# Weights one piece later and a reordered block inverse in the RWKV stage of a hybrid diffusion step

## The chip, the cores and the metric

One core of one Trainium2 chip. The metric is the device time of one launch in microseconds: median 2254.62 us of three runs before the change (2253.39 to 2256.46).

## The reference, cut to what matters

One layer over 640 tokens (512 of a sample, 128 of a prompt), model width 2048. A normed and modulated input goes through one large projection `w_in`; an RWKV-7 branch (16 heads of 64 channels, scanned forward and backward) and an RG-LRU branch run beside each other, are projected, gated, summed, projected once more, added to the input and normed.

```python
def rwkv7_scan(r, w, k, v, kk, a, s0, reverse):
    def step(s, inp):
        r_t, w_t, k_t, v_t, kk_t, a_t = inp
        s_kk = jnp.einsum('bhvk,bhk->bhv', s, kk_t)
        s = s * w_t[:, :, None, :] - s_kk[..., None] * (kk_t * a_t)[:, :, None, :] + v_t[..., None] * k_t[:, :, None, :]
        return s, jnp.einsum('bhvk,bhk->bhv', s, r_t)
    ...
    z = xm @ p['w_in']
    r, k, v, g_a, x_b, g_b, m_a, m_b = jnp.split(z, SPLITS, axis=-1)
    ...
    (y_f, bo_f, s_f), (y_bk, bo_bk, s_bk) = dirs_a
    y_rwkv = head_group_norm((y_f + y_bk)...) + (bo_f + bo_bk).reshape(bsz, t, W_A)
    y_a = (y_rwkv.astype(dt) * jax.nn.silu(g_a)) @ p['w_out_a']
    merged = jax.nn.sigmoid(m_a) * y_a + jax.nn.sigmoid(m_b) * y_b
    out = merged @ p['w_out']
```

The kernel computes the scan in chunks of 64 tokens. Within a chunk the steps form a triangular system (I + A), and the kernel inverts that matrix for each of 10 chunks, 2 directions and 2 heads of a channel tile.

## The kernel before

**Stages.** Modulation and norm, the RG-LRU branch (to about 500 us), the RWKV branch (to about 1765 us), the branches' output projections with the merge, and the last projection with the final norm. Products with weights run on TensorE in float32 as three products of two exact parts each.

**Pieces of weights.** The stream of weights is cut into pieces of 128x512 (4 k-tiles of one column tile, 256 KB). SyncE issues the load of a piece into one of 3 raw tiles `wr` (`fetch`, line 297). `split` turns each half of a piece into a high part `wh` (ScalarE, line 309) and a low part `wl` (GpSimd, line 310), with 5 tiles of each. `piece` (line 327) runs 4 k-tiles on TensorE, 6 matmuls of 320 columns each. Before every half-piece it first splits up to 5 half-pieces ahead and then calls `fetch(pos[1] // 2 + src["raw"])`, so that loads stand 3 pieces ahead of the split in the program.

**Ticks.** After each k-tile comes one tick: it counts down the delayed calls (`later(n, fn)`) and lets three queues of generators (front, side, back) run one step each. `yield from idle(n)` waits n ticks. Ticks fix in which order instructions stand on an engine; each engine then runs its own list strictly in that order and waits where it must. All DMAs spoken of here are issued by SyncE (the rows' SPq), so a load stands behind whatever was issued before it in the program.

**The RWKV stage** has 8 channel tiles, numbered 0 to 7. While `rwkv(i, v)` runs for tile i, the products of the next tile's r, k, v, of a gate and of some merge gates go through the pieces: 28 pieces for each of tiles 1 to 6. For one tile, `rwkv` does in this order:

- `first` (line 968): products whose masked result `at` holds A, forward (d = 0) and then backward (d = 1).
- `send` (line 1011): four DMAs write the 32x32 diagonal blocks of A to DRAM; they are read back with one block on each partition, forward into `xn` (line 1079) and backward into `xi` (line 1098). ScalarE turns the forward blocks (line 1102: `xi` from `xn`) and the backward ones (line 1105: `xn` from `xi`).
- The elimination: 30 steps of two VectorE instructions each (lines 1110 and 1112) invert all blocks, while `second` and `turned` go on TensorE between. The tuples `W` and `INV` hold the ticks between these steps. It ends with a memset of the diagonal (line 1118) and a turned copy to `xn` (line 1119).
- Four DMAs (line 1123) send `xi` and `xn`, each for both directions, to DRAM. `QI[1]` ticks later four small loads (line 1131) bring what the first products need, and eight (line 1137) bring the diagonal blocks of the full inverse `qm`. `QI[2]` ticks after that follow the first products of the inverse (line 1146), copied by ScalarE at line 1152, 3 ticks later the second products (line 1160), copied at line 1166, and then the recurrence over chunks.

Behind the elimination the next tile's `normed` starts: it loads two tiles `th` (line 821) and squares `nk` (line 902).

Of the kernel before, what the change touches and what calls it, by code (L numbers as in the profile page):

```python
# [9 lines left out]
F32 = mybir.dt.float32  # L10
# [6 lines left out]
P = 128  # L17
D = 2048
KT = D // P            # 16 k-tiles of the model dimension
WA = 1024  # L20
NT = WA // P           # 8 channel tiles of a branch
TS = 512               # sample tokens
TP = 128               # prompt tokens
T = TS + TP            # 640 tokens: sample first, then prompt
HT = T // 2            # tokens of one PSUM half
CH = 64                # chunk of the RWKV recurrence
NC = T // CH           # 10 chunks: 8 of the sample, 2 of the prompt
LR = 96
EARLY = 2              # column tiles of w_in among the first products
NS = 3 + EARLY         # and with those of the LoRA branches  # L30
SLOT = 658             # columns of a slot: 640 tokens with the borders of their shifts
NM = (5, 3, 3, 3, 3, 3, 4)          # column tiles of the merge gates among the products of a channel tile
CUT = 350              # tokens of the first group of the output projection
# buffers: parts of weights, the same and raw weights of the last phase, ada_w, gate's weights, slots of the LRU phase
WB, EW, ER, ADAB, GS, LS = 5, 5, 6, 10, 2, 14
# The order in which TensorE takes the work that others wait for, in pieces of the products between its steps.
# start: steps behind each group of ada_w; loads of ada_w before the first weights; place of the derived parameters
LQ = ((), (0, 2, 3, 5, 7), (4, 6, 8), (1, 3, 4, 6, 8), (1, 3, 4, 6, 8), (1, 3, 4, 6, 8), (1, 4, 4, 6, 8), (1, 3, 4, 6, 8))
LF, DN = 2, 0
# LRU phase: LoRA, convolution, gates, recurrence, gate's third of the modulation  # L40
# [3 lines left out]
# RWKV phase: keys' side; chunk products, inverses, recurrence; group norm  # L44
QB, NQ, HP, BC, BG = 21, 7, (4, 3, 3), 5, 2
W = (2, 2, 2, 2, 2, 2, 2, 2, 2, 1, 3, 2)
INV = (0, 1, 1, 1, 1, 1, 1, 1, 2, 2, 2, 2, 2, 2, 2, 2)
QI = (1, 5, 7, 3, 1)
# [4 lines left out]
# output projections  # L53
# [5 lines left out]
# per-channel parameters of the two branches, in the order in which they are packed  # L59
# [3 lines left out]
# columns of the constants  # L63
# [3 lines left out]
HB = CH // 2           # blocks that VectorE inverts  # L67
NB = 4 * NC            # of them in a direction of a channel tile
# [15 lines left out]
def _lay_out(inp):  # L84
    """The inputs as the kernel reads them: transposed, tiled and packed, no arithmetic."""
# [14 lines left out]
    # the column tiles of the first products, in pieces of 2 k-tiles, k-tiles outermost, two to a transfer  # L100
# [5 lines left out]
    # shift and scale: tile of columns, third, group of 4 k-tiles, partition, k-tile, column  # L106
    w = f["ada_w"][0][:, :2 * D].reshape(4, 4, P, 2, KT, P)
    a["ada_w"] = w.transpose(4, 3, 0, 2, 1, 5).reshape(KT, 2, 4, P, 4 * P)
    # gate: half of k, tile of columns, column, k
# [25 lines left out]
def step_kernel(ctx: ExitStack, tc: tile.TileContext, xt, w_in, w_a, w_b, w_o, ws, lw2, ada_w, ada_g, ada_b, cond, condr, gains,  # L135
# [17 lines left out]
    # ---------------------------------------------------------------- constants and parameters  # L153
# [3 lines left out]
    blk = keep.tile([P, P], F32R, name="blk")        # ones between the channels of a head  # L157
# [4 lines left out]
    mod = keep.tile([P, 3, KT, 2], F32, name="mod")      # shift, 1 + scale (times the norm's gain), gate  # L162
# [13 lines left out]
    def derive(pool):  # L176
        V.tensor_scalar(dv[:, 0:3], pt[:, 0:3], -1.0, 1.0, ALU.mult, ALU.add)          # 1 - mu
        V.tensor_scalar(dv[:, 3:6], pt[:, 0:3], 0.25, None, ALU.mult)                  # mu / 4
        V.tensor_scalar(dv[:, 6:9], pt[:, 0:3], 0.5, None, ALU.mult)                   # mu / 2
        kb = PAR.index("dw0")  # L180
        V.tensor_scalar(dv[:, 9:17], pt[:, kb:kb + 8], 0.5, None, ALU.mult)            # halved biases of the sigmoids
        V.tensor_scalar(dv[:, 17], pt[:, PAR.index("k_a")], 0.5, None, ALU.mult)
        V.tensor_scalar(dv[:, 18], pt[:, PAR.index("k_k")], -1.0, None, ALU.mult)
        # 4 softplus(-lambda), softplus(-l) = max(-l, 0) + 2 atanh(e / (2 + e)), e = exp(-|l|)
# [18 lines left out]
    # ---------------------------------------------------------------- side work, between the pieces of the products  # L203
# [43 lines left out]
    # ---------------------------------------------------------------- the stream of weights  # L247
    # Each piece: 4 k-tiles of one column tile, split exactly into two parts of 12 significant bits.
# [41 lines left out]
    src = {"pool": wpool, "raw": 3, "parts": WB}  # L290
# [9 lines left out]
    def split(j):  # L300
        """Parts up to half-piece j."""
        while pos[1] < min(j, 2 * len(stream)):
            k, q = divmod(pos[1], 2)
            r = raws[k][:, 2 * P * q:2 * P * (q + 1)]
            if q:
                raws.pop(k)
            h = src["pool"].tile([P, 2 * P], F32R, tag="wh", name="wh", bufs=src["parts"])
            lo = src["pool"].tile([P, 2 * P], F32R, tag="wl", name="wl", bufs=src["parts"])
            S.activation(h, r, AF.Copy)  # L309
            lows[pos[1] % len(lows)].tensor_tensor(lo, r, h.bitcast(F32), ALU.subtract)  # L310
            parts[pos[1]] = (h, lo)
            pos[1] += 1

    def piece(j, xs, hs, k0, nk, ticks=True, qs=range(4)):
        """p[m, tokens a to b] += (4 k-tiles of the weights)^T @ x, both in two parts, for (p, a, b) of hs."""
        for q in qs:
            if q % 2 == 0:
                split(2 * j + q // 2 + src["parts"])
                fetch(pos[1] // 2 + src["raw"])
# [25 lines left out]
    def newton(x, y, t):  # L345
        """x^-1/2 from x > 0 and the table's value y for it: one step, to y."""
# [8 lines left out]
    # ---------------------------------------------------------------- modulation and the normed input  # L355
# [9 lines left out]
    def ada_load(pool, bufs, t):  # L365
        """Group t of 4 k-tiles of 2 column tiles of ada_w, by pair of column tiles, third and k."""
# [17 lines left out]
    def ada_turn(third, n, ms, psa):  # L384
        """To 2 channel tiles of mod, the four groups of columns summed, with the bias."""
# [6 lines left out]
    with tc.tile_pool(name="start", bufs=1) as st, tc.tile_pool(name="ps", bufs=2, space=PSUM) as sp:  # L392
# [40 lines left out]
        # the first column tiles: two are summed in PSUM, the others in sums  # L433
# [7 lines left out]
        def modulated(n):  # L441
            """The normed and modulated input of 2 channel tiles."""
# [14 lines left out]
        def first(n, c):  # L457
            """Column tile c's products with 2 channel tiles."""
# [62 lines left out]
    # ---------------------------------------------------------------- LoRA branches and the RG-LRU branch  # L521
# [5 lines left out]
    with tc.tile_pool(name="lru", bufs=1) as lp:  # L527
# [19 lines left out]
        def parted(src, name, low, bufs=1):  # L547
            """Two parts of 12 significant bits."""
# [5 lines left out]
        def small(p, w, x):  # L554
            """p = w^T @ x, both in two parts."""
# [43 lines left out]
        def lru(i, xb, sg):  # L599
# [32 lines left out]
            for d in range(2):  # L632
                # log a = -4 sp (1 + th);  1 - a^2 = tanh(-log a) (1 + a^2)
# [38 lines left out]
        def gates():  # L672
            """The gate's third of the modulation: columns on partitions, sums over k along them."""
# [35 lines left out]
        for i in range(NT):  # L709
            side.append(lora(i))  # L710
            xb = slot("xb")
            # sample: 2 zeros, 512, 1 zero; prompt: 2 zeros, 128, 1 zero
# [16 lines left out]
            V.scalar_tensor_tensor(halves(sg), halves(sg), 1.0, ps[:, :, :HT], ALU.add, ALU.mult)   # 2 silu(g_b)  # L729
# [9 lines left out]
    # ---------------------------------------------------------------- the RWKV branch  # L739
# [3 lines left out]
    with tc.tile_pool(name="rwkv", bufs=1) as rp:  # L743
# [3 lines left out]
        def mixed(q, i):  # L747
            """The projection of r, k or v, mixed with its shift."""
# [47 lines left out]
        # (I + A)^-1, transposed, of each chunk: its blocks of 32 from VectorE, the rest from TensorE  # L796
# [4 lines left out]
        NV = 64 + NB       # partitions that hold blocks, backward from 64  # L801
# [620 lines left out]
```

## Time and profile before

| | |
|---|---|
| median of 3 runs | 2254.62 us (2253.39 to 2256.46) |
| span of the profiled execution | 2255.7 us, 1.1 us above the median and within the range of the runs |
| busy: TensorE / VectorE / ScalarE / GpSimd | 94% / 60% / 43% / 39% |
| DMA | 38.9% of 16 engines' time on SyncE's queue |
| chain that ended last | TensorE 67%, VectorE 20%, DMA 4% |

The profile lists busy time, waits ("idle before, and who ended it") and the instructions in order of time. Where an engine's row has [6.05 <-DMA xi<-scr], the engine stood idle for 6.05 us until that DMA landed. A row merges neighbours of one kind: x4 behind it is their number, and its duration runs from the first to the last.

### The profile page before, as it was taken

What the parts mean: (1) busy time and instruction counts of PE and PEld (TensorE: products, weight loads), DVE (VectorE), ACT (ScalarE), POOL (GpSimd) and SP (SyncE); (2) the same over time, 40 slices, a digit from 0 to 9 for tenths busy, and PEclk for the clock granted to TensorE, in tenths of its full rate; (3) what the DMA queues carried; (4) which work ended last, traced back from release to release, by engine and by line L of the source; (5) the groups of instructions that cost most, each with busy time, mean ns of one, the idle gap of its engine ahead of it and who ended that gap; (6) DMA issues with size and microseconds to landing.
All of it is one profiled execution on the core that took longest, in us unless ns stands there. A gap on an engine that the chain in (4) does not pass through costs nothing.

```text
span 2255.7 us, 47335 instructions
## 1 busy us (share of the span) xinstructions
PE 2115.5 (94%) x18236; PEld 1971.3 (87%) x18236; DVE 1346.7 (60%) x2536; ACT 980.9 (43%) x2264; POOL 890.8 (39%) x1164
## 2 busy tenths in 40 slices
PE   4999898999999899898998998989999999999997
PEld 2788898998888889798898897888988899999997
DVE  5557898968856667656756676567362422223364
ACT  4336566653434443433443434334433422234554
POOL 1245555664323333333333433333323444443343
PEclk8999899999999999999999999999999999999999
DMA  8955555432322322322222223222232533345574
GB/s 334 349 175 166 177 174 173 155 101 85 96 82 72 87 70 72 99 78 78 78 83 86 68 76 97 71 74 92 85 90 68 196 122 122 122 143 159 153 237 151
DMA packets 198609, 281.63 MB, mean 125 GB/s; under 512 B 68816, under 2 KB 90512, under 8 KB 197616
## 3 DMA queue, kind: packets, MB, share of 16 engines
q1 hardware_dynamic: 197936, 277.38, 38.9%
q8 instruction: 144, 2.36, 0.4%
q0 software_dynamic: 448, 1.23, 0.2%
q14 instruction: 81, 0.66, 0.1%
HBM read 237.70 MB, written 39.85 MB: 123 GB/s over the span
## 4 chain that ended last, share of the span: by engine, by line
PE 67%; DVE 20%; DMA 4%; issue 2%; ACT 2%; SPq 1%; POOL 0%; DVEq 0%; ACTq 0%; POOLq 0%
PE pj L327 50%; DVE tmp L1110 3%; DVE xi L1112 3%; PE rw L557 2%; PE rw L968 2%; PE rw L473 2%; DVE st L992 2%; DVE xc L611 1%; DMA scr<-xn 1%; PE pj L473 1%; PE rw L1191 1%; PE rw L1179 1%; PE rw L1204 1%; DVE gws L703 1%; PE ada L375 1%
## 5 line engine op out<-in xcount | busy, mean ns | idle before, releaser
L310 POOL TENSOR_TENSOR wl<-wr,wh 128x256 fp32r<-128x256 f32 x922 | 804.5, 880 | 1266.7 <-ACT wh L309 1223.9
L327 PE MATMUL pj<-xh,wh 128*128 128x320 f32 (+2 forms) x2976 | 764.6, 325 | 2.4 <-ACT wh L309 2.4
L327 PE MATMUL pj<-xh,wl 128*128 128x320 f32 (+2 forms) x2976 | 726.2, 312 | 1.9 <-DVE wl L310 1.4
L327 PE MATMUL pj<-xl,wh 128*128 128x320 f32 (+2 forms) x2976 | 726.3, 312 | 0.0
L309 ACT ACTIVATE wh<-wr 128x256 fp32r<-128x256 f32 x1048 | 423.6, 413 | 547.2 <-PE pj L327 421.0
L327 PEld LDWEIGHTS pj<-xh,wh 128*128 128x128 f32 x2976 | 503.3, 190 | 34.3 <-issue 14.2
L327 PEld LDWEIGHTS pj<-xh,wl 128*128 128x128 f32 x2976 | 513.7, 190 | 3.7 <-DVE wl L310 2.1
L327 PEld LDWEIGHTS pj<-xl,wh 128*128 128x128 f32 x2976 | 514.9, 190 | 0.1
L1110 DVE TENSOR_TENSOR tmp<-xn,xi 104x30 f32<-104x30 f32 (+14 forms) x240 | 102.7, 428 | 82.0 <-ACT xn L1105 75.5
L1039 DVE COPY sv<-rw 64x128 f32<-64x128 f32 x80 | 23.6, 294 | 197.2 <-ACT sv L1038 196.1
L310 DVE TENSOR_TENSOR wl<-wr,wh 128x256 fp32r<-128x256 f32 x126 | 58.4, 465 | 125.0 <-ACT wh L309 124.8
L1112 DVE TENSOR_TENSOR xi<-xi,tmp 104x30 f32<-104x30 f32 (+14 forms) x240 | 100.0, 416 | 8.2
L1338 DVE SCALAR_TENSOR_TENSOR thx<-thx,pj 128x640 f32<-128x640 f32 x16 | 13.2, 823 | 95.8 <-PE pj L327 95.8
L992 DVE TENSOR_TENSOR st<-rw,c 64x512 f32<-64x512 f32 (+1 forms) x96 | 57.5, 599 | 12.4 <-PE rw L986 10.2
L327 PE MATMUL pj<-ybh,wl 128*128 128x320 f32 x256 | 58.6, 310 | 0.4 <-POOL wl L310 0.3
L327 PE MATMUL pj<-ybh,wh 128*128 128x320 f32 x256 | 58.5, 310 | 0.0
L327 PE MATMUL pj<-yah,wh 128*128 128x320 f32 x256 | 58.4, 309 | 0.0
L327 PE MATMUL pj<-yah,wl 128*128 128x320 f32 x256 | 58.4, 309 | 0.0
L327 PE MATMUL pj<-yal,wh 128*128 128x320 f32 x256 | 58.3, 309 | 0.0
L327 PE MATMUL pj<-ybl,wh 128*128 128x320 f32 x256 | 58.3, 309 | 0.0
L1146 PE MATMUL rw<-xi,at 32*32 32x32 f32 x640 | 15.0, 231 | 43.4 <-DMA xi<-scr 42.9
L1038 ACT ACTIVATE sv<-rw 64x128 f32<-64x128 f32 x80 | 21.6, 271 | 75.9 <-PE rw L1191 70.2
(766 smaller groups left out, 3168.2 us busy)
## 6 DMA issues: line engine op xcount, KB each, us to landing
wr<-w_in SPq DMA_DIRECT2D x312, 256.0 KB
adaw<-ada_w SPq DMA_DIRECT2D x64, 512.0 KB
wr<-w_o SPq DMA_DIRECT2D x128, 256.0 KB
gws<-ada_g SPq DMA_DIRECT2D x32, 512.0 KB
thl<-th SPq DMA_DIRECT2D x32, 320.0 KB
th<-thl SPq DMA_DIRECT2D x32, 320.0 KB
thm<-g SPq DMA_DIRECT2D x64, 160.0 KB
thx<-thm SPq DMA_DIRECT2D x32, 320.0 KB
```

Source lines behind the costliest of these rows:

```text
L309: S.activation(h, r, AF.Copy)
L310: lows[pos[1] % len(lows)].tensor_tensor(lo, r, h.bitcast(F32), ALU.subtract)
L327: PE.matmul(p[:, :t1 - t0], w, x[:, t0:t1], start=(k == 0 and a == 0), stop=(k == nk - 1 and a == 2))
L375: PE.matmul(pm[32 * q:32 * q + 32, :2 * P].rearrange("p (b c) -> p b c", b=2), sc[:, 4 * g + q], wt[:, :, P * q:P * (q + 1)], start=(g == ...
L473: PE.matmul(p[:, :HT], u[:, w], x[:, t], start=new, stop=end)
L557: PE.matmul(p, a, b, start=(n == 0), stop=(n == 2))
L611: V.scalar_tensor_tensor(xc[:, a:b], xb[:, o + q:o + q + n], pc(f"cw{q}", i), xc[:, a:b], ALU.mult, ALU.add)
L968: PE.matmul(pa[hd(e), x:x + P], z.bk[d][hd(e), n, e], st4s[d][hd(e), n, e].rearrange("p a t -> p (a t)"), start=True, stop=True)
L992: V.tensor_tensor(st4s[d][so, n0:n0 + nn, e], pb[so, :m].rearrange("p (c a t) -> p c a t", a=2, t=CH), mb[so], ALU.mult)
L1039: V.tensor_copy(sv[hd(1), a, 1], src[hd(1), b])
L1110: V.tensor_tensor(t, xn[:NV, j, j + 1:].unsqueeze(2).to_broadcast([NV, m, j]), xi[:NV, j, :j].unsqueeze(1).to_broadcast([NV, m, j]), ALU.mult)
L1112: V.tensor_tensor(xi[:NV, j + 1:, :j], xi[:NV, j + 1:, :j], t, ALU.add)
```

## The change

Four edits in the RWKV stage; the comments fall away too. Loads of weights are called 2 instead of 3 pieces ahead from the start of the RWKV stage to the end of the merge, with the same 3 raw tiles. The forward blocks of A are sent one tick sooner, read back 5 ticks sooner and turned 5 ticks sooner; the backward blocks are sent, read back and turned one tick sooner each, and the elimination starts 2 ticks sooner in the program and gets 2 ticks more. The four sends after it go in another order, and the 12 small loads are called 2 ticks sooner.

```diff
-W = (2, 2, 2, 2, 2, 2, 2, 2, 2, 1, 3, 2)
-INV = (0, 1, 1, 1, 1, 1, 1, 1, 2, 2, 2, 2, 2, 2, 2, 2)
-QI = (1, 5, 7, 3, 1)
+W = (2, 2, 2, 2, 2, 2, 2, 2, 2, 1, 2, 1)
+INV = (0, 1, 1, 1, 1, 1, 1, 2, 2, 2, 2, 2, 2, 2, 2, 3)
+QI = (1, 3, 9, 3, 1)
...
-    src = {"pool": wpool, "raw": 3, "parts": WB}
+    src = {"pool": wpool, "raw": 3, "ahead": 3, "parts": WB}
...
-                fetch(pos[1] // 2 + src["raw"])
+                fetch(pos[1] // 2 + src["ahead"])
...
-            later(2, lambda: send(0))
+            later(1, lambda: send(0))
...
             pb = heads([z.bonus])
+            later(1, lambda: nc.sync.dma_start(xn[0:NB], sa[0][0].rearrange("g n r c -> (g n) r c")))
             yield from idle(W[5])
...
-            later(2, lambda: send(1))
-            later(2, lambda: nc.sync.dma_start(xn[0:NB], sa[0][0].rearrange("g n r c -> (g n) r c")))
+            later(1, lambda: send(1))
+            later(3, lambda: nc.sync.dma_start(xi[64:NV], sa[1][0].rearrange("g n r c -> (g n) r c")))
+            S.activation(xi[0:NB], xn[0:NB].rearrange("p j t -> p t j"), AF.Copy)
...
             yield from idle(W[8])
-            nc.sync.dma_start(xi[64:NV], sa[1][0].rearrange("g n r c -> (g n) r c"))
             next(work)
             yield from idle(W[9])
             next(work)
-            S.activation(xi[0:NB], xn[0:NB].rearrange("p j t -> p t j"), AF.Copy)
             yield from idle(W[10])
-            next(work)
             S.activation(xn[64:NV], xi[64:NV].rearrange("p t j -> p j t"), AF.Copy)
+            next(work)
             yield from idle(W[11])
...
-            for d in range(2):
-                for w, x in ((1, xi), (2, xn)):
-                    nc.sync.dma_start(sa[d][w].rearrange("g n r c -> (g n) r c"), x[64 * d:64 * d + NB])
+            for d, w in ((0, 1), (1, 2), (1, 1), (0, 2)):
+                nc.sync.dma_start(sa[d][w].rearrange("g n r c -> (g n) r c"), (xi, xn)[w - 1][64 * d:64 * d + NB])
...
+        src.update(ahead=2)
         pace[:] = [0.0, 1.0]
         rkv = {}
...
-        src.update(pool=fp, raw=ER, parts=EW)
+        src.update(pool=fp, raw=ER, ahead=ER, parts=EW)
```

Three places in the order of the instructions. The numbers behind names tell the buffers apart; a piece of weights is the same tile `wr_...` on SyncE (its load) and on ScalarE (its split).

SyncE (SP) behind the four sends of tile 1's inverse, before:

```order
L297 DMA wr_8711<-w_in 128x512
L1131 DMA xi_5437<-scr1_0_1_5426 32x10x32 x2
L1131 DMA xi_5437<-scr1_1_2_5430 32x10x32 x2
L1137 DMA qm0_5434<-scr1_0_2_5427 32x10x32 x2
L1137 DMA qm1_5435<-scr1_1_1_5429 32x10x32 x2
L1137 DMA qm0_5434<-scr1_0_2_5427 32x10x32 x2
L1137 DMA qm1_5435<-scr1_1_1_5429 32x10x32 x2
L821 DMA th_8765<-thl2_0_1688 128x640
L821 DMA th_8767<-thl2_2_1690 128x640
L297 DMA wr_8777<-w_in 128x512
```

Ahead of the 12 small loads stands one piece, behind the loads of `th` the next. ScalarE (ACT) at the same place before, from the wait for `nk` to the copies behind the first products:

```order
L902 ACTIVATE q_8771<-nk_8769 128x640
L309 ACTIVATE wh_8773<-wr_8592 128x256
L309 ACTIVATE wh_8791<-wr_8657 128x256
L309 ACTIVATE wh_8807<-wr_8657 128x256
L309 ACTIVATE wh_8825<-wr_8711 128x256
L1152 ACTIVATE xn_5436<-rw_8835 32x320 x2
L1152 ACTIVATE xn_5436<-rw_8836 32x320 x2
```

The piece whose first half ScalarE splits right before line 1152 (wr_8711) is loaded ahead of the 12 small loads. SyncE at the same place now:

```order
L297 DMA wr_8709<-w_in 128x512
L1131 DMA xi_5437<-scr1_0_1_5426 32x10x32 x2
L1131 DMA xi_5437<-scr1_1_2_5430 32x10x32 x2
L1137 DMA qm0_5434<-scr1_0_2_5427 32x10x32 x2
L1137 DMA qm1_5435<-scr1_1_1_5429 32x10x32 x2
L1137 DMA qm0_5434<-scr1_0_2_5427 32x10x32 x2
L1137 DMA qm1_5435<-scr1_1_1_5429 32x10x32 x2
L821 DMA th_8763<-thl2_0_1688 128x640
L821 DMA th_8765<-thl2_2_1690 128x640
L297 DMA wr_8775<-w_in 128x512
```

What stands between the two pieces is unchanged; which pieces they are, ScalarE's rows now tell:

```order
L902 ACTIVATE q_8769<-nk_8767 128x640
L309 ACTIVATE wh_8771<-wr_8655 128x256
L309 ACTIVATE wh_8789<-wr_8709 128x256
L309 ACTIVATE wh_8805<-wr_8709 128x256
L309 ACTIVATE wh_8823<-wr_8775 128x256
L1152 ACTIVATE xn_5436<-rw_8833 32x320 x2
L1152 ACTIVATE xn_5436<-rw_8834 32x320 x2
```

The piece split right before line 1152 is now wr_8775, and its load stands behind the 12 small loads and the two loads of `th`. ScalarE before the elimination of tile 1, before:

```order
L309 ACTIVATE wh_8197<-wr_8010 128x256
L1005 ACTIVATE tok_7889<-rw_8218 128x5x64
L1005 ACTIVATE tok_7889<-rw_8219 128x5x64
L1102 ACTIVATE xi_5437<-xn_5436 40x1024
L309 ACTIVATE wh_8233<-wr_8077 128x256
L1272 ACTIVATE g_8249<-pj_7873 128x320
L309 ACTIVATE wh_8251<-wr_8077 128x256
L1105 ACTIVATE xn_5436<-xi_5437 40x1024
```

The same stretch now (lines 1102 and 1105 have become 1082 and 1104):

```order
L1082 ACTIVATE xi_5437<-xn_5436 40x1024
L1272 ACT_TABLE_LOAD
L1272 ACTIVATE g_8175<-pj_7871 128x320
L309 ACTIVATE wh_8178<-wr_8079 128x256
L309 ACTIVATE wh_8197<-wr_8079 128x256
L1005 ACTIVATE tok_7887<-rw_8217 128x5x64
L1005 ACTIVATE tok_7887<-rw_8218 128x5x64
L309 ACTIVATE wh_8231<-wr_8141 128x256
L1272 ACTIVATE g_8247<-pj_7871 128x320
L1104 ACTIVATE xn_5436<-xi_5437 40x1024
```

The forward turn has moved ahead of a merge gate, two halves of weights and the copies of `tok`, and the backward turn has one instruction of 128x256 less ahead of it.

## Rows read from the trace of the kernel before

**Rows 1.** The page, part 1: the span and TensorE's busy time.
```profile
span 2255.7 us, 47335 instructions
...
PE 2115.5 (94%) x18236; PEld 1971.3 (87%) x18236; DVE 1346.7 (60%) x2536; ACT 980.9 (43%) x2264; POOL 890.8 (39%) x1164
```
**Rows 2.** TensorE's waits: who waited for whom, total us, times, longest us.
```profile
PE rw L1146 <- DMA xi<-scr: 42.9, 16, 6.5
```
**Rows 3.** TensorE's timeline, tile 1 and tile 6: start, duration, instruction, [idle before].
```profile
752.96 0.46 PE L327 MATMUL pj<-xh,wh 128*128 128x320 f32 x2
753.25 0.46 PE L327 MATMUL pj<-xl,wh 128*128 128x320 f32 x2
...
760.04 0.82 PE L1146 MATMUL rw<-xi,at 32*32 32x32 f32 x6 [6.05 <-DMA xi<-scr]
761.21 1.27 PE L1146 MATMUL rw<-xi,at 32*32 32x32 f32 x74 [0.34 <-DMA xi<-scr]
...
762.41 0.90 PE L327 MATMUL pj<-xh,wh 128*128 128x320 f32 x2
...
767.11 0.89 PE L1160 MATMUL rw<-qm,xn 32*32 32x32 f32 x80
...
1522.54 0.89 PE L1160 MATMUL rw<-qm,xn 32*32 32x32 f32 x80
```
**Rows 4.** Busy time and granted clock (PEclk) behind tile 1's first products.
```profile
761.00:767.00 6.00, 5.79 (x92) 5.65 (x92) 0.00 (x0) 2.75 (x6) 3.06 (x4) 0.54 0.55 117
```
**Rows 5.** VectorE's timeline: elimination's start and end, tile 1; its end, tile 6.
```profile
716.47 0.19 DVE L1110 TENSOR_TENSOR tmp<-xn,xi 104x30 f32<-104x30 f32 x1 [9.10 <-ACT xn L1105]
...
752.95 0.09 DVE L1118 MEMSET xi<- 104x32 f32 x1
...
1509.43 0.09 DVE L1118 MEMSET xi<- 104x32 f32 x1
```
**Rows 6.** ScalarE's timeline in tile 1: the turns, the halves, line 1152.
```profile
711.26 2.09 ACT L1102 ACTIVATE xi<-xn 40x1024 f32<-40x1024 f32 x1
...
714.33 2.10 ACT L1105 ACTIVATE xn<-xi 40x1024 f32<-40x1024 f32 x1
...
758.87 1.38 ACT L309 ACTIVATE wh<-wr 128x256 fp32r<-128x256 f32 x4
762.44 1.78 ACT L1152 ACTIVATE xn<-rw 32x320 f32<-32x320 f32 x4 [2.19 <-PE rw L1146]
```
**Rows 7.** SyncE's timeline in tile 1, behind the four sends.
```profile
755.67 0.86 SPq L297 DMA_DIRECT2D wr<-w_in  x1
756.58 3.02 SPq L1131 DMA_DIRECT2D xi<-scr  x4
759.69 4.73 SPq L1137 DMA_DIRECT2D qm<-scr  x8
764.47 0.93 SPq L821 DMA_DIRECT2D th<-thl  x2
765.50 2.19 SPq L297 DMA_DIRECT2D wr<-w_in  x3
```
**Rows 8.** SyncE in tile 6, behind the loads of th: the issue.
```profile
1522.26 1.72 SPq L297 DMA_DIRECT2D wr<-w_in  x3
```
**Rows 9.** ScalarE's halves that waited for a load: tiles 6, 7, end of stage.
```profile
1526.13 0.42 ACT L309 ACTIVATE wh<-wr 128x256 fp32r<-128x256 f32 x1 [0.48 <-DMA wr<-w_in]
...
1677.30 0.42 ACT L309 ACTIVATE wh<-wr 128x256 fp32r<-128x256 f32 x1 [5.62 <-DMA wr<-w_in]
...
1771.70 0.42 ACT L309 ACTIVATE wh<-wr 128x256 fp32r<-128x256 f32 x1 [3.89 <-DMA wr<-w_in]
```
**Rows 10.** SyncE at the end of the stage: the loads behind five loads of yr.
```profile
1765.56 0.85 SPq L297 DMA_DIRECT2D wr<-w_in  x2
```
**Rows 11.** TensorE in tile 0: a wait of the stage, and the second products.
```profile
602.93 0.61 PE L892 MATMUL rw<-qhh,blk 128*128 128x320 f32 x1 [3.04 <-ACT g L1272]
...
619.76 0.89 PE L1160 MATMUL rw<-qm,xn 32*32 32x32 f32 x80
```

More of the change, by code (lines that the diff above doesn't have):

```diff
@@ L1101, in rwkv @@
             next(work)
-            S.activation(xi[0:NB], xn[0:NB].rearrange("p j t -> p t j"), AF.Copy)
             yield from idle(W[10])
+            S.activation(xn[64:NV], xi[64:NV].rearrange("p t j -> p j t"), AF.Copy)
             next(work)
-            S.activation(xn[64:NV], xi[64:NV].rearrange("p t j -> p j t"), AF.Copy)
             yield from idle(W[11])
```

## The prediction, made before the changed kernel ran

> **What bounds the kernel now.** I read the busy shares first: TensorE works 94% of a span of 2255.7 us [rows 1], so time can only go or come where TensorE stands. The list of its waits then names one large wait of the RWKV stage: 42.9 us ahead of the first products of the inverse, for the small loads of line 1131 [rows 2]. In the timeline of tile 1 it is one piece: 6.05 and 0.34 us ahead of line 1146, with the main part of these products at 761.21 and the second products (line 1160) at 767.11 [rows 3]. Tiles 1 to 6 look alike, tiles 0 and 7 are treated apart.
>
> Next I followed that wait back. VectorE ends the elimination at 752.95, and it had stood idle for 9.10 us until the backward turn let it begin at 716.47 [rows 5]. So the elimination starts when ScalarE's line 1105 is done (714.33 + 2.10), and line 1102 (2.09 us at 711.26) stands shortly ahead of that [rows 6]. Behind the elimination SyncE issues, one after another, a piece of weights, 12 small loads, two loads of `th` and the next weights [rows 7]. I count from the end of the elimination before, E = 752.95: small loads from E + 3.6, the load behind `th` at E + 12.6, first products E + 8.3, second products E + 14.2; in tile 6 the second products come at 1522.54 - 1509.43 = 13.1 [rows 3, 5]. As the middle of these six I take E + 13.6.
>
> **The change part by part.**
>
> *Earlier blocks.* Line 1102 leaves the place ahead of the backward turn (2.09 us), and one half of weights goes behind it. On the other side a merge gate and the copies of `tok` still stand ahead of it, so I take 2.2 us for the start of the elimination. The bounds are 0 (its data come no sooner) and 9.10 (all of VectorE's idle time). VectorE has the same 60 steps and the same other work between, so the end moves by as much: E - 2.2.
>
> *Order of the sends.* The third and fourth small load need the backward `xn`, which was sent last and now goes second. The four issues took 3.02 us where eight later ones took 4.73 [rows 7]: 4 x 0.59 = 2.4, so 0 to about 1.2 us can go; I take 0.6. The earlier call of the small loads (`QI[1]`) passes nothing on SyncE in tiles 1 to 6: the same number of weight loads, one, stands between sends and small loads.
>
> By these two parts the first products come at E + 8.3 - 2.8 = E + 5.5. That is 2.8 us of TensorE's wait in each tile, were it all.
>
> *Weights one piece later.* In general I cost this at nothing: there are still 3 raw tiles, a load still waits for the same tile to be free, and the splits run up to five half-pieces ahead. A half-piece is 6 pairs of matmuls at 0.29 us [rows 3], 1.8 us, so five are about 8.8 us of cover. What was queued behind a waiting weight load goes out sooner. What now stands behind other SyncE work is a weight load, and at one place the cover is gone. ScalarE splits a half-piece right ahead of line 1152, the copies that the second products need. Before, that piece was loaded ahead of the 12 small loads (755.67, E + 2.7). Now one piece less has been fetched, and that load is the one behind the small loads and `th` (765.50) [rows 7]. Its issue is E + 12.6 - 2.8 = E + 9.8. In tile 6 the load in this slot was issued at 1522.26 [rows 8] and the half that waited for it began at 1526.13 [rows 9]: 3.9 us. So the piece is there at E + 13.7, the half takes 0.42, line 1152 takes 1.78 [rows 6], and the second products start about 0.1 later, at E + 16.0. Before it was E + 13.6. Each of the six tiles loses 2.4 us, although its first products came 2.8 us sooner: 6 x 2.4 = 14.4 us. Queued behind ScalarE's waiting half are line 1152, the square of the next tile and all later halves; behind TensorE's line 1160 is everything.
>
> The Trainium skill, "DMA: Bandwidth & Descriptors", section "Anatomy of one DMA", fits a transfer as about 2.0 us and its bytes over 436 GB/s, which would be an estimate of 2.6 us for a piece of 256 KB. The row says 3.9 us in this slot, behind two loads of 320 KB, and the measurement decides. By the page the loss would be 1.1 us a tile, 6.6 us in all. The same page's "Rules for kernel authors" say to issue a transfer early and wait for it late, which speaks against this part; how late is too late no page says, and the sum stands without it.
>
> *The clock.* After the idle time of 6 us, TensorE was granted 0.54 of its speed from 761 to 767, the lower of its two levels (1.2 GHz) for most of it [rows 4]. The three k-tiles between first and second products took 767.11 - 762.41 = 4.7 us, against 9 x 0.29 = 2.6 at the upper level (2.4 GHz) [rows 3]: 2.1 us lost, inside the E + 13.6. Now there are two idle times: about 3.6 us (6.39 - 2.8) ahead of the first products, and then, with these done at about E + 6.7 and three k-tiles of 2.6 to 4.7 us, 4.6 to 6.7 us ahead of the second ones. What the clock loses after the first is hidden in the second; after the second nothing hides it. I take 2.1 us again, 6 x 2.1 = 12.6 us, with bounds 0 and 0.46 x 6.0 = 2.8 us a tile.
>
> *Tile 0* has no `th` in between, and loses its wait of 3.04 us at 602.93 in part, as a store comes out sooner; but its second products (619.76) [rows 11] then wait for a load that is also behind the 12 small ones. I take +2 (bounds -3 and +5). *Tile 7*: ScalarE waited 5.62 us for this very load even before [rows 9], when it was issued ahead of the small ones; now it is behind them, while the elimination ends sooner. I take +1 (bounds -1 and +6).
>
> *End of the stage.* Two weight loads at 1765.56 stood behind five loads of `yr` [rows 10], and the split of the first waited until 1771.70 [rows 9]. One piece less is there beforehand, so TensorE runs dry one piece sooner: 12 pairs x 0.29 = 3.5 us. I take +4 with some clock (bounds 0 and +6).
>
> Sum: 14.4 + 12.6 + 2 + 1 + 4 = 34 us on 2255.7. That execution stood 1.1 us above the median of 2254.62, so 2254.6 + 34 = 2288.6, told as 2288 us.
>
> **The rivals.**
>
> 1. *The clock does not fall a second time* (0.22). The shortened first wait may leave it up, or the second end before it falls. For it: the bound of 0. Against: an idle time of 6 us was followed by the low level in rows 4. Time: 2288 - 12.6 = 2275.
>
> 2. *The elimination ends no sooner* (0.09). The backward turn may be held by its data or by the halves ahead. Then the second products come at E + 18.2, 2.2 us later still in six tiles: 2288 + 13 = 2301.
>
> 3. *Gain and loss cancel* (0.06): the load lands in the page's 2.6 us, no second fall of the clock, nothing at the end: 2254.6 + 6.6 - 3 = 2258 and below, about 2255.
>
> 4. *Faster, because the elimination starts much sooner* (0.13). The second products hang on its end: they come as early as before where it ends 2.2 + 2.4 = 4.6 us sooner, and earlier from there. For it: VectorE's 9.10 us of idle time, and a forward turn that now is far ahead, so that only the backward one counts. Against: that one still stands behind a gate and halves of weights that wait for TensorE's own progress, and it moved by one tick only. At 9.10 us the gain is 4.5 us a tile in seven tiles, 31 us, so about 2223; a middle case is 2240.
>
> **How the numbers follow.** The forecast has 0.50, and with rivals 1 and 2 slower has 0.81. A measurement of this kernel tells a change from none at about 0.2%, 4.5 us: same is 2250 to 2259, where rival 3 lies: 0.06. Faster is rival 4: 0.13. The low end takes 6.6 us for the loads, no second clock loss and -3 of tile 0: 2258. The high end takes 2.8 us for the clock (+4), +5, +6 and +6 for the three single places (+10), no gain by the order of the sends (+4): 2306. Outside lie rival 4 and a little of both ends.
>
> **What would show it.** Right: TensorE's wait at line 1146 shrinks to 3 or 4 us a tile; a new wait of 4 to 7 us appears ahead of line 1160; ScalarE's half ahead of the copies of line 1152 is ended by a load of weights; the granted clock is low behind the second products. VectorE's idle time ahead of the elimination is about 7 us instead of 9.10. The last forward pieces of the stage show a longer wait near 1766. Wrong: line 1152 follows the first products at once, as it did, or the elimination starts 5 us or more sooner; then tiles get shorter and the kernel faster.

## The result and the profile after

The changed kernel takes 2295.62 us (median of 4 runs, 2292.84 to 2296.55) against 2255.54 us (2253.39 to 2257.10) for the kernel before: a ratio of 1.017, 95% interval 1.0158 to 1.0183, so about 40 us slower. The forecast was 2288 us, with 2258 to 2306 as its range and slower as the likeliest side. The profiled execution has a span of 2293.5 us, 37.8 more than [rows 1].

TensorE's waits in the changed kernel (who waited for whom, total us, times, longest us), against the one wait of [rows 2]:

```profile
PE rw L1160 <- ACT xn L1152: 38.0, 13, 5.3
PE rw L1146 <- DMA xi<-scr: 25.4, 9, 4.1
...
PE pj L327 <- ACT wh L309: 4.9, 1, 4.9
```

The old wait shrank from 42.9 to 25.4 us, and a new one of 38.0 us stands behind it, ahead of line 1160. In tile 1 TensorE's timeline (start, duration, instruction, [idle before]) shows both, where [rows 3] had one:

```profile
760.27 0.34 PE L1146 MATMUL rw<-xi,at 32*32 32x32 f32 x4 [4.08 <-DMA xi<-scr]
760.77 1.36 PE L1146 MATMUL rw<-xi,at 32*32 32x32 f32 x76 [0.17 <-DMA xi<-scr]
762.06 0.90 PE L327 MATMUL pj<-xh,wh 128*128 128x320 f32 x2
...
765.41 0.46 PE L327 MATMUL pj<-xh,wl 128*128 128x320 f32 x2
770.85 0.29 PE L1160 MATMUL rw<-qm,xn 32*32 32x32 f32 x2 [4.98 <-ACT xn L1152]
771.30 2.17 PE L1160 MATMUL rw<-qm,xn 32*32 32x32 f32 x78 [0.17 <-ACT xn L1152]
```

TensorE runs the three k-tiles between the two products and then stands still for 4.98 us. Behind it line 1160 itself takes 2.17 us where it took 0.89. Who holds it is read from ScalarE's timeline of the same place; [rows 6] has the same instructions before:

```profile
758.32 0.74 ACT L902 ACTIVATE q<-nk 128x640 f32<-128x640 f32 x1 [9.84 <-DVE nk L900]
758.97 0.40 ACT L309 ACTIVATE wh<-wr 128x256 fp32r<-128x256 f32 x1
759.93 0.72 ACT L309 ACTIVATE wh<-wr 128x256 fp32r<-128x256 f32 x2 [0.57 <-DMA wr<-w_in]
769.92 0.42 ACT L309 ACTIVATE wh<-wr 128x256 fp32r<-128x256 f32 x1 [9.27 <-DMA wr<-w_in]
770.36 1.79 ACT L1152 ACTIVATE xn<-rw 32x320 f32<-32x320 f32 x4
```

Before, four halves stood together and line 1152 waited only for TensorE. Now three halves go, and the fourth waits 9.27 us for a load of weights, with line 1152 queued behind it, although its products were done at about 762.1. The load is the first of the three that SyncE issues last here:

```profile
755.76 1.10 SPq L297 DMA_DIRECT2D wr<-w_in  x1
756.91 2.42 SPq L1131 DMA_DIRECT2D xi<-scr  x4
759.42 4.97 SPq L1137 DMA_DIRECT2D qm<-scr  x8
764.43 0.93 SPq L821 DMA_DIRECT2D th<-thl  x2
765.46 1.32 SPq L297 DMA_DIRECT2D wr<-w_in  x3
```

The order on SyncE is that of [rows 7]; what differs is which piece each load of weights brings. The half that waits for the first of these three starts 4.46 us after that load's issue (765.46 to 769.92).

On VectorE the idle time ahead of the elimination is 6.69 us where it was 9.10 [rows 5], and the elimination's end is at 753.02:

```profile
716.26 0.19 DVE L1110 TENSOR_TENSOR tmp<-xn,xi 104x30 f32<-104x30 f32 x1 [6.69 <-ACT xn L1104]
...
753.02 0.09 DVE L1118 MEMSET xi<- 104x32 f32 x1
```

TensorE came to line 1146 at 760.27 - 4.08 = 756.2, so 3.2 us behind that end; before it came at 760.04 - 6.05 = 754.0, 1.0 us behind the end of 752.95. By TensorE's progress the elimination thus ends 2.1 us sooner.

The granted clock stands in the windows (from and to in us, length, busy time of PE, PEld, DVE, ACT, POOL, then PEclk, DMA share, GB/s). In the changed kernel, first between the first and the second products, then behind the second ones:

```profile
762.00:769.00 7.00, 3.87 (x24) 3.54 (x18) 0.00 (x0) 0.00 (x0) 0.00 (x0) 0.85 0.65 169
...
771.70:778.00 6.30, 6.11 (x118) 5.46 (x119) 0.00 (x0) 4.31 (x10) 2.98 (x3) 0.52 0.17 56
```

and in the kernel before, behind its second products at 767.11:

```profile
768.00:775.00 7.00, 7.00 (x94) 6.22 (x96) 1.48 (x4) 4.87 (x12) 1.47 (x2) 1.00 0.35 122
```

So the clock is low a second time, at 0.52 (the 1.2 GHz level nearly throughout), where it was at its full 2.4 GHz before. Its price is read over equal work, 123 matmuls from the first of line 1160 on, in the kernel before and in the changed one:

```profile
767.11:770.77 3.66, 3.66 (x123) 3.36 (x123) 0.00 (x0) 2.69 (x7) 0.39 (x2) 1.00 0.78 276
...
770.85:778.13 7.28, 6.83 (x123) 5.92 (x124) 0.00 (x0) 5.14 (x12) 3.27 (x4) 0.53 0.16 52
```

TensorE's busy time grows by 3.2 us; the rest of the 3.6 us are short waits of line 1160 between the copies of line 1152.

What the waits and the clock are worth together is read from the five tiles between the second products of tile 1 and those of tile 6. The kernel before:

```profile
767.11:1522.54 755.43, 715.51 (x7252) 648.87 (x7251) 496.53 (x1050) 315.30 (x775) 262.76 (x390) 0.98 0.27 80
```

and the changed one:

```profile
770.85:1554.35 783.50, 729.72 (x7250) 660.04 (x7251) 499.27 (x1050) 317.46 (x776) 263.59 (x391) 0.96 0.26 77
```

The same work takes 28.1 us longer, 5.6 us a tile. TensorE is idle for 53.8 instead of 39.9 us (+13.9), and its busy time grows by 14.2 us over an equal number of instructions: half of the loss is waiting, half is longer work, as the lower clock made it in tile 1 (3.2 us more behind the second products, and less than before ahead of them).

Tile 0, tile 7's first products and the end of the stage, TensorE in the changed kernel (before, tile 0: [rows 11]):

```profile
600.32 0.38 PE L892 MATMUL rw<-qhh,blk 128*128 128x320 f32 x1 [0.80 <-DVE st L992]
...
619.23 0.24 PE L1160 MATMUL rw<-qm,xn 32*32 32x32 f32 x2 [3.72 <-ACT xn L1152]
...
1709.38 1.53 PE L1146 MATMUL rw<-xi,at 32*32 32x32 f32 x80 [1.09 <-DMA xi<-scr]
...
1801.04 0.46 PE L327 MATMUL pj<-xh,wl 128*128 128x320 f32 x2
1806.41 0.90 PE L327 MATMUL pj<-xh,wh 128*128 128x320 f32 x2 [4.92 <-ACT wh L309]
...
1812.53 0.45 PE L327 MATMUL pj<-xh,wh 128*128 128x320 f32 x2
```

and in the kernel before:

```profile
1677.50 0.38 PE L1146 MATMUL rw<-xi,at 32*32 32x32 f32 x4 [3.40 <-DMA xi<-scr]
...
1765.32 0.46 PE L327 MATMUL pj<-xh,wl 128*128 128x320 f32 x2
...
1772.17 0.55 PE L327 MATMUL pj<-xh,wh 128*128 128x320 f32 x2 [2.35 <-ACT wh L309]
```

Counted by TensorE's matmuls of line 327, of which both kernels have equally many in the same order, 1765.32 and 1801.04 are the same matmul, and so are 1772.17 and 1812.53. The wait at the end thus stands 24 matmuls, one piece, sooner in the program than before.

### The profile page after: what moved, and what is told of

Its sections match the earlier page's. It is cut to its first block, busy times and chain, and to the rows that moved or that the text cites. A ratio compares the mean times of both kernels' runs of the same rounds, so it can differ in the third digit from the quotient of the medians.

```text
span 2293.5 us, 47346 instructions
## 1 busy us (share of the span) xinstructions
PE 2131.9 (93%) x18236; PEld 1984.7 (87%) x18236; DVE 1345.8 (59%) x2536; ACT 984.5 (43%) x2264; POOL 895.1 (39%) x1164
## 3 DMA queue, kind: packets, MB, share of 16 engines
q1 hardware_dynamic: 197936, 277.38, 37.8%
## 4 chain that ended last, share of the span: by engine, by line
PE 64%; DVE 23%; DMA 5%; ACT 3%; SPq 3%; issue 3%; POOL 0%; DVEq 0%; ACTq 0%; POOLq 0%
PE pj L327 47%; DVE tmp L1110 4%; DVE xi L1112 4%; DMA wr<-w_in 2%; PE rw L473 2%; PE rw L968 2%; DVE st L992 2%; PE rw L557 2%; SPq L1137 2%; PE pj L473 1%; PE rw L1179 1%; DVE xc L611 1%; PE ada L375 1%; PE rw L1191 1%; PE rw L1204 1%
## 5 line engine op out<-in xcount | busy, mean ns | idle before, releaser
L1160 PE MATMUL rw<-qm,xn 32*32 32x32 f32 x640 | 17.3, 237 | 40.7 <-ACT xn L1152 38.0
```

## The experiments

The theory from here on, called L: only the distance of the loads costs time. It sets which piece ScalarE splits right ahead of line 1152, and where that piece is loaded behind the small loads and `th`, the second products wait for it. The other parts of the change gain. Ratios are to the kernel before, run on the same chip.

**e1_three_ahead**: the changed kernel with the old distance.

```diff
-        src.update(ahead=2)
+        src.update(ahead=3)
```

> The changed kernel with the loads of weights called 3 pieces ahead again; all else of the change stays. Theory L (the late load): the loss hangs on the piece whose load stands behind the 12 small loads and th. With it back ahead of them, line 1152 follows the first products at once: no wait ahead of the second products (line 1160) in tiles 1 to 6, about 4 us ahead of the first ones as in the changed kernel, and the kernel becomes faster than before by some 3 us a tile and a shorter low clock: about 2232 us (2222 to 2242). Rival M (the moves): the turns, ticks and the new order of the sends cost the time, by the earlier copies on ScalarE and by the inverse standing otherwise; then the wait ahead of the second products stays and the time is 2280 us or more. Rival H (half and half): near 2255, the earlier blocks gain nothing.

Measured: 2241.03 us, ratio 0.9929 (0.9908 to 0.9951). No wait ahead of line 1160 is left, and that of line 1146 is as in the changed kernel, about 4 us a tile (6.4 us in tile 5):

```profile
PE rw L1146 <- DMA xi<-scr: 28.2, 8, 6.4
```

Line 1152 again waits for TensorE's products alone, here 1.79 us, and no longer for a half:

```profile
763.33 1.79 ACT L1152 ACTIVATE xn<-rw 32x320 f32<-32x320 f32 x4 [1.79 <-PE rw L1146]
```

L holds. The gain is 15 us, not 24: it is as large as the wait that went (42.9 - 28.2 = 14.7). The forecast's shorter low clock did not come: TensorE's busy time is 2118.1 us in this profile and 2115.5 us in that of [rows 1], and a wait of 4 us still stands in each tile.

**e2_only_ahead**: the kernel before with nothing but the shorter distance.

```diff
-    src = {"pool": wpool, "raw": 3, "parts": WB}
+    src = {"pool": wpool, "raw": 3, "ahead": 3, "parts": WB}
...
-                fetch(pos[1] // 2 + src["raw"])
+                fetch(pos[1] // 2 + src["ahead"])
...
+        src.update(ahead=2)
...
-        src.update(pool=fp, raw=ER, parts=EW)
+        src.update(pool=fp, raw=ER, ahead=ER, parts=EW)
```

> The kernel before with one edit alone: loads of weights called 2 pieces ahead from the start of the RWKV stage. Theory L: the elimination ends as before, the load behind the small ones is as late as in the changed kernel, so the second products of tiles 1 to 6 come about 4.5 us later than before, with a low clock behind them, and the end of the stage loses 3 us: 2300 us (2288 to 2312), slower than the whole change. TensorE waits 6 us ahead of line 1146 and 4 to 5 us ahead of line 1160. Rival M: no wait ahead of line 1160, 2255 us within 5.

Measured: 2309.51 us, ratio 1.0238 (1.0220 to 1.0256), with both waits in TensorE's list:

```profile
PE rw L1146 <- DMA xi<-scr: 42.1, 16, 6.4
PE rw L1160 <- ACT xn L1152: 32.0, 11, 5.5
```

With e1 this makes a square of four kernels. The distance costs 53.1 us alone (2256.4 to 2309.5) and 54.6 us with the rest of the change (2241.0 to 2295.6); the rest gains 15.4 or 13.9 us. The two effects add: the 40 us are +54 and -14. (The 2295.6 us come from another series, whose kernel before took 0.8 us less.)

**e3_load_first**: the changed kernel, with the next piece fetched ahead of the small loads.

```diff
             yield from idle(QI[1])
+            fetch(pos[1] // 2 + 3)
```

> The changed kernel with one more call of a weight load ahead of the 12 small loads in each tile; elsewhere the loads stay 2 pieces ahead. Theory L: the one load explains tiles 0 to 7, so the wait ahead of line 1160 goes in all of them; the small loads come 0.4 to 1 us later; the end of the stage keeps its loss of 3 us: about 2237 us (2226 to 2248). Rival M: 2280 us or more. If loads being late elsewhere in the stage counted too, it would lie well above the run with all loads 3 pieces ahead.

Measured: 2245.37 us, ratio 0.9948 (0.9933 to 0.9963). One load a tile, moved past the small loads, takes away the whole wait at line 1160 (line 1161 here) and leaves 4.8 to 5.2 us ahead of the first products, as the small loads come that much later. Line 1152 (1153 here) follows its products at once:

```profile
756.98 1.78 ACT L1153 ACTIVATE xn<-rw 32x320 f32<-32x320 f32 x4 [1.56 <-PE rw L1147]
```

So it is the position of that single load, not the number of loads in flight.

**e4_th_later**: the changed kernel, with the loads of `th` issued behind the weights instead of ahead of them.

```diff
             z = Scan(i, k, r)
-            z.load(0)
...
             yield from idle(NQ)
+            z.load(0)
```

> The changed kernel with the two loads of th (320 KB each) called 7 ticks later, so that the next weights stand right behind the 12 small loads. Theory L: the load is issued 1.0 us sooner and lands in 2.5 to 3.5 us instead of 4.4, so line 1160 starts 2 to 2.5 us sooner in tiles 1 to 6, tiles 0 and 7 as in the changed kernel: about 2281 us (2274 to 2287). Rival: the 12 small loads themselves, or what stands behind them on the DMA engines, hold the second products; then no change, 2295 us.

Measured: 2275.33 us, ratio 1.0083 (1.0066 to 1.0100). The half ahead of line 1152 waits 6.67 instead of 9.27 us, and TensorE's waits ahead of and in line 1160 fall from 38.0 to 23.8 us (19.9 listed under `xn`, 3.9 under loads):

```profile
766.54 0.42 ACT L309 ACTIVATE wh<-wr 128x256 fp32r<-128x256 f32 x1 [6.67 <-DMA wr<-w_in]
...
763.48 0.88 SPq L297 DMA_DIRECT2D wr<-w_in  x2
764.41 0.90 SPq L821 DMA_DIRECT2D th<-thl  x2
```

The load is issued 1 us sooner, and its half starts 3.06 instead of 4.46 us behind the issue. Tiles 0 and 7 have no `th` ahead of that load; in tiles 1 to 6, summed from the timeline, TensorE's waits at line 1160 go from 29.8 to 15.8 us. There `th` is thus about half of the new wait, and what is left is gone in e3, where the load stands ahead of the 12 small ones too. The gain was larger than forecast, within the range.

**e5_old_send_order**: e1, with the four sends in their old order.

```diff
-            for d, w in ((0, 1), (1, 2), (1, 1), (0, 2)):
+            for d, w in ((0, 1), (0, 2), (1, 1), (1, 2)):
```

> Loads three pieces ahead as in e1_three_ahead (2241 us), and the four sends of xn in their old order again. My theory: the third and fourth small load then wait for the backward xn that is sent last, so the products of line 1146 start about 0.5 us later in tiles 1 to 6, some 3.5 us in all: about 2244 (2239 to 2249), with TensorE's wait ahead of line 1146 at 4.5 us a tile where it was 4.0. Rival: the order of the sends hides nothing, since the small loads are issued one after another anyway: 2241 and 4.0 us a tile.

Measured: 2240.41 us, ratio 0.9927 (0.9915 to 0.9940), no different from e1's 0.9929. The wait ahead of line 1146 grows by 2.6 us in all (30.8 us, against 28.2). The wait moved the way that the theory on record told, by 2.6 of 3.5 us; in the time, the order of the sends cannot be told from no change.

**e7_earlier_end**: e1, with the backward turn and all steps of the elimination one tick sooner. The last tuple value puts a tick more behind the last step, so that the memset and the sends keep their tick; the text on record names only the last steps.

```diff
-W = (2, 2, 2, 2, 2, 2, 2, 2, 2, 1, 2, 1)
-INV = (0, 1, 1, 1, 1, 1, 1, 2, 2, 2, 2, 2, 2, 2, 2, 3)
+W = (2, 2, 2, 2, 2, 2, 2, 2, 2, 1, 1, 1)
+INV = (0, 1, 1, 1, 1, 1, 1, 2, 2, 2, 2, 2, 2, 2, 2, 4)
```

> Loads three pieces ahead, and the elimination's last steps put one tick sooner. If the path in each tile runs from the end of the elimination over the sends and small loads to line 1146, its end comes about 0.9 us sooner for TensorE in seven tiles: about 2235 (2229 to 2241), and the wait ahead of line 1146 falls from 4.0 to about 3.1 us. Rival: VectorE is held by its own work and the last steps only come as they can: 2241, with the same waits. On the other side: with a step more in the tick, VectorE's other work (the st of line 992, the masks) comes later and TensorE waits there, 2245.

Measured: 2235.99 us, ratio 0.9911 (0.9897 to 0.9924): the time that was forecast, but its interval overlaps with e1's. The waits ahead of line 1146 did not fall as expected (28.5 us in all, 2.4 to 6.5 us a tile), so the step on which the forecast stood is not shown. By TensorE's progress the end came sooner in tiles 1 and 4, where TensorE reaches line 1146 4.98 and 3.80 us behind it (3.17 in e1), and later in tiles 2, 3 and 6 (2.13).

**e8_four_more**: e1, with line 1146 called four ticks later in all tiles but the last.

```diff
-            yield from idle(QI[2])
+            yield from idle(QI[2] + (4 if i < NT - 1 else 0))
```

> Loads three pieces ahead, and line 1146 called four ticks later (ten instead of six pieces of cover), all tiles but the last. Theory L (what decides is which piece of weights ScalarE splits right ahead of line 1152, and whether its load stands behind the small loads and th): the halves ahead of line 1152 then belong to the piece whose load is behind th, so the wait ahead of line 1160 comes back at 2 to 5 us, and the time is about 2255 (2240 to 2270). Rival (more cover hides more): the 4.0 us ahead of line 1146 go and nothing comes for them, 2211 (2205 to 2222).

Measured: 2281.25 us, ratio 1.0117 (1.0101 to 1.0132). More cover for the first products makes the kernel slower by 40 us against e1. The wait of line 1146 goes in tiles 0 to 6, and these come in TensorE's list:

```profile
PE rw L1160 <- ACT xn L1152: 21.9, 16, 3.7
...
PE pj L327 <- ACT wh L309: 18.0, 7, 3.7
```

In tile 2 ScalarE shows the same trap with the distance of three, since line 1152 now stands behind a half of the next piece:

```profile
926.28 0.42 ACT L309 ACTIVATE wh<-wr 128x256 fp32r<-128x256 f32 x1 [6.24 <-DMA wr<-w_in]
926.72 1.77 ACT L1152 ACTIVATE xn<-rw 32x320 f32<-32x320 f32 x4
```

L told the sign and place; the time lies above its range (2240 to 2270), since the forecast had no place for the second list entry, halves that come late ahead of line 327.

**e9_th_behind_two_more**: e1 with e4's edit and `QI[2] + 2` in place of e8's `+ 4`.

> Loads three pieces ahead, the loads of th issued behind the next weights instead of ahead of them, and line 1146 called two ticks later. Theory L: the piece that is split ahead of line 1152 was loaded ahead of the small loads, and the one behind it no longer waits for th, so nothing comes back ahead of line 1160; line 1146 has two pieces more of cover and waits about 2.0 us instead of 4.0: 6 x 2 = 12 less than 2241, about 2229 (2222 to 2240). Rival: th then comes late for its first reader, or a wait ahead of line 1160 of 1 to 2 us returns: 2241 to 2250.

Measured: 2240.76 us, ratio 0.9930 (0.9917 to 0.9942), no gain over e1 and above the range that L gave (2222 to 2240). As L has it, nothing waits at line 1160, and line 1146 waits in tile 7 alone. But other waits of TensorE came in their place (of the last, 3.5 us were there in the kernel before):

```profile
PE pj L327 <- ACT wh L309: 15.1, 8, 2.3
PE rw L1200 <- DVE sv L1039: 11.3, 12, 1.5
PE rw L968 <- DVE st L874: 8.7, 7, 3.1
```

The first of them comes from ScalarE's square of the next tile, which holds up the halves behind it until VectorE has made `nk`, whose instruction stands behind the elimination:

```profile
758.01 0.74 ACT L901 ACTIVATE q<-nk 128x640 f32<-128x640 f32 x1 [9.84 <-DVE nk L899]
758.65 1.32 ACT L309 ACTIVATE wh<-wr 128x256 fp32r<-128x256 f32 x4
```

**e11_square_later**: e9 with that square three ticks later.

```diff
+            yield from idle(3)
             S.activation(q[:, :T], nk[:, :T], AF.Square)
-            yield from idle(NQ)
+            yield from idle(NQ - 3)
```

> As e9_th_behind_two_more (2241 us), and ScalarE's square of the key (line 902, 9.84 us of waiting for VectorE's nk that stands behind the elimination) called three ticks later, so that in tiles 1 to 6 two halves of weights more are split ahead of it. My theory: the waits of TensorE for a half ahead of line 327 (2.35 us in most tiles, 15.1 us in all) are what the more cover turned into, and they go: 2241 - 13 = 2228 (2222 to 2236). Rival: the tile's length hangs on a chain that runs through VectorE's elimination and not on TensorE's cover, so the waits only move on, to line 1146 or to lines 1200 and 968: 2237 to 2243.

Measured: 2245.83 us, ratio 0.9953 (0.9938 to 0.9969). The waits for halves go, and TensorE, which so comes to the first products sooner, waits there again (line 1147 here):

```profile
PE rw L1147 <- DMA xi<-scr: 19.6, 10, 3.2
```

The waits only moved on, as the rival had it; the time is a little above the rival's 2237 to 2243. That the length of a tile now comes from the elimination's end, and not from TensorE's cover, is argued here; e12 tests it.

**e12_and_earlier_end**: e11 with e7's two tuples, so with the turn and the elimination's steps one tick sooner.

> As e11_square_later, with the elimination's last steps one tick sooner as in e7_earlier_end, which gave 4 to 5 us there. Theory: where the waits are gone already, an earlier end has less to give: 2226 (2220 to 2234). Rival (the chain through the elimination sets the length of a tile): the 4.5 us come off again, 2233 to 2237.

Measured: 2234.91 us, ratio 0.9905 (0.9888 to 0.9921), within the rival's range, and 11 us below e11 where the intervals do not touch. The rival had told 4.5 us from a lower start, so its value is in part luck; its direction is shown. By TensorE's progress the elimination ends sooner in tiles 2, 4 and 6, where TensorE reaches the first products 6.74 us behind that end (3.87 to 4.96 in e11). The wait is down again:

```profile
PE rw L1147 <- DMA xi<-scr: 11.4, 10, 3.2
```

It is the fastest version run, faster than both kernels, but not told apart from e7, which has three edits less (the place of `th`, the two ticks, the square).

## Why the prediction was right

- *The trap at line 1152*, the step that carried the sign, happened as described: same half, same load, same queue behind it. e1, e2 and e3 show it by taking the distance back, by making it alone, and by moving the one load.
- *Its size.* The second products of tiles 1 to 6 start at E + 17.8 in the mean (16.6 in tile 6, 17.8 to 18.2 in the others), with E this kernel's own end of elimination; 2.1 us sooner than before, so E + 15.7 on the prediction's count against the 16.0 worked out. Before it was 13.6: 2.1 us lost against 2.4. Three errors are inside, and that they nearly cancel is luck. The load took 4.46 us in the row above (3.9 assumed), and SyncE came to it at E + 12.4 (12.0). Against these, the prediction let the second products wait for the whole of line 1152 and 0.1 us more, 1.88 us; line 1160 starts 0.49 us behind the start of line 1152 (770.85 against 770.36), when the first of its four copies can be done. The estimate of 2.6 us by the Trainium skill, "DMA: Bandwidth & Descriptors", section "Anatomy of one DMA", whose fit is for transfers that GpSimd issues, falls 1.9 us short of this load, which SyncE issued.
- *The clock* was the term that was mis-sized: 2.1 us a tile assumed, 3.2 us measured over equal work behind tile 1's second products, with 0.4 us of short waits beside it. Its bounds went to 2.8. From tile 1's second products to tile 6's a tile takes 5.6 us longer, of which 5.6 - 2.1 = 3.5 us are left for what lies behind the second products, so tile 1 is no exception. The window with 0.52 shows the second fall itself, rival 1's opposite. The Trainium skill, "TensorE: Matmul & The Clock Gate", section "HAM oscillation — how this bites in real kernels", tells of a loop whose every pass pays for the lower clock anew, since its products are shorter than the wait for data; it advises to do more products between waits. The windows here agree in that each tile pays anew: over five tiles the first wait shrank, a second one came, and both together cost as much busy time (+14.2 us) as idle time (+13.9 us).
- *Earlier blocks*: 2.2 us assumed for the end of the elimination, 2.1 measured; VectorE's idle time 6.69 us, about 7 told. *Order of the sends*: 0.6 us assumed. The main part of the first products came at E + 8.3 before and at 760.77 - 753.02 = 7.75 now, so 0.5; e5 puts its worth for the time at none that can be told.
- *Tile 0*: its second products start 0.5 us sooner (619.23 against [rows 11]), as the wait of 3.04 fell to 0.80 and the 3.72 us ahead of line 1160 took most of that back. But line 1160 and what stands behind it then run slower, and TensorE comes to tile 1's line 1146 2.2 us later than before (756.2 against 754.0). That is the +2 assumed.
- *Tile 7 and the end.* TensorE comes to tile 7's line 1146 34.2 us later than before (1709.38 - 1.09 against 1677.50 - 3.40), to the matmul ahead of the wait at the stage's end 35.7 us later (1801.04 against 1765.32), and the span ends 37.8 us later. So tile 7 took 1.5 us (+1 assumed) and the end 2.0 us (+4 assumed). TensorE runs dry one piece sooner, as told, but the wait is only 2.6 us longer (4.92 against 2.35), where 3.5 us of work were counted as lost.
- *Rivals.* 1 and 2 fall by the clock's window and by the 2.1 us. 3 falls with the loss. 4 asked for 4.6 us sooner at the end of the elimination. Its condition did not come, but its direction is e1: without the trap the same earlier start makes the kernel 15 us faster.

The sum of 34 us came out at 37.8 between the profiled spans. Tiles 1 to 6 took 34.2 - 2.2 = 32.0 us where 14.4 + 12.6 = 27.0 were told; the clock's term is what was too small in them, and the end of the stage, 2.0 us too large, hid part of it.

## What to carry to other kernels

Where an engine splits weights and copies results in one strict list, ask for each copy which load the instruction ahead of it waits for, and what that load is queued behind. A prefetch distance is such a choice, not only a depth: one piece less put a 256 KB load behind 12 small ones and turned a gain of 14 us into a loss of 40, and moving that one load alone got it back (e3). Cover added at one wait (e8, e9) and a square moved away (e11) only moved the wait to another instruction. No run here shows that such cover pays: e9 is no faster than e1, and e12, where the elimination ends sooner in some tiles, is not told apart from e7, which has no added cover.

## What the runs showed of the hardware

- In the kernel before, one idle time of 6 us was followed by a granted clock of 0.54 from 761 to 767 [rows 4] and of 1.00 from 768 on. In the changed one, an idle time of 4 us was followed by 0.85 from 762 to 769, and a second one of 5 us, with 5.6 us of products between the two, by 0.52 over 6.3 us. The two waits cost more than the one, by 2.8 us of waiting and 2.8 us of longer work a tile.
- The half that waited for a weight load of 256 KB started 4.46 us after the load's issue, where two loads of 320 KB stood right ahead of it; in e4, with these two behind it, 3.06 us.
- ScalarE waited 9.84 us ahead of the square of line 902 (901 in e9) in the changed kernel and in e9. In the changed kernel TensorE's list has no wait for it; in e9 TensorE then waited up to 2.35 us for the halves queued behind it.
